# A fp32 hybrid decoder layer on one core: the embedding's early units loaded and split sooner, the second group's values built sooner and half by half, the last partial sum added in PSUM

## The chip, the core and the metric

One NeuronCore of a Trainium2 chip. The metric is device time of one execution in microseconds (us), lower is better. The engines are TensorE (PE; PEld is its weight load), VectorE (DVE), ScalarE (ACT), GpSimd (POOL) and SyncE (SP, which here only issues DMAs).

## The reference

One layer over 1024 tokens of width 2048, all in fp32:

```python
h = x @ w_in + b_in
q, k, v, g_attn, u_pool, g_pool = split(h)          # 16 heads of 64, 2 KV groups of 8 heads
a = banded_sink_attention(q, k, v, sinks, rel_bias) * silu(g_attn)   # window 128, blocks of 128
b = multiscale_pool(u_pool, w_pool, pool_scale) * silu(g_pool)       # trailing means 2, 4, 8, 16
mix = concat(a, b) @ w_out
ple = sigmoid(x @ w_gate_ple) * (p @ w_ple)         # p: (1024, 256), w_ple: (256, 2048)
out = layer_norm(sqrt(2) * x + mix + ple, gain, bias)
```

## The kernel before

**Matmuls.** A product of two fp32 matrices is made of three matmuls in the type fp32r (`mm3`, lines 182 to 184): each operand is split into hi (a cast on ScalarE, line 728) and lo (a subtraction on VectorE, line 125), and the matmuls are hi·hi, hi·lo and lo·hi. The big products run in groups of a Strassen-like scheme (`run_group`, `product`): a group has the seven products p1, p2, p5, p6, p7, p3, p4 in this order, each for up to three jobs, and each `product` is 12 matmuls of 512 columns. Its left operands are units of the input (b11, b21, t1 = sums of b12 and others, t2, t3, t4, b22, in hi and lo tiles such as `t1h`, `t1l`), its right ones slices of the weights (`raw`, sums of them in `s`, split into `wh`, `wl`). Units are loaded, summed and split some products ahead of their use (`units_to(i + 4)`).

**Order.** The code is written in the order of the work; `tick()` counts products, `after(t, f)` and `later(d, f)` hang a piece of work on a count. A tile scheduler then fixes the order of instructions on each engine. Within an engine, instructions run in order. SP's loads go out in order, and each waits for the landing of the load eight before it.

**The start.** `first()` in `run` loads the first operands. While they arrive, TensorE multiplies four of the embedding's eight units early (`EARLY = (0, 1, 6, 7)`; here n = 0 to 3): `ple_load` loads two units of `w_ple` at once into a `two` tile (512 KB), `ple_split(n)` splits one (casts on ScalarE at line 767, subtractions on VectorE) into the tiles that later hold t3 (`t3h`, `t3l`), and `ple_half(n, h)` multiplies one half of the tokens (12 matmuls; p lies in `t4h`, `t4l`) into the PSUM banks `tr` and `pv` and copies them to `b22h` or `b22l`. Units 2 and 3 (`ple_load(3)` loads both) are worked between the products of group 0: `turn` puts `ple_half(2, 0)`, (2, 1), (3, 0), (3, 1) ahead of the p5 products of the three jobs and of the first p6. `p5` products go to the PSUM bank `qb` and `sc`, p6 to `qa`.

**Heads.** A second part of the matmuls runs interleaved with the attention heads (`heads(h, j)`: 16 calls, two halves of the tokens, h, for each of 8 pairs). `v_build(g, src)` makes for each half h of the tokens a tile `v0` or `v1` from the stored values (`src`, loaded by POOL from `kv`): transposes on TensorE (line 522), a cast on ScalarE (524), a subtraction on VectorE; the products with the probabilities (line 625, into `pv`) read it. For KV group 0 it is made ahead of the heads, for group 1 in between, at tick t + 63 + 22, both halves from one call.

**The tail.** The last jobs are plain products (`run_plain`, 256 columns, F2). Their results are sums of a part in SBUF (`new_part`) and PSUM; `less_mean` (line 905) subtracts the mean with one more matmul. `norm_square` squares each block (ScalarE, line 915), `norm_scale` sums the squares on TensorE (924), makes 1/std (942 and a power on POOL) and spreads it over PSUM (957). `norm_out_two` multiplies eight pairs of blocks by it on VectorE, scales each by gain and bias (the pair's first block on ScalarE, its second on an engine that is given, line 975; `None` is ScalarE) and stores it (SP, 256 KB each).

Of the kernel before, what the change touches and what calls it, by code (L numbers as in the profile page):

```python
# [32 lines left out]
T = 512  # L33
# [7 lines left out]
Q0, KB, VB, GA0, U0, GP0 = 0, 8, 9, 10, 18, 26  # L41
# [23 lines left out]
class Layer:  # L65
# [80 lines left out]
    def fetch(self, src, extra=False):  # L146
        s = self.extra() if extra else self.slot()
        return self.load(s[:, : src.shape[-1]], src)
# [17 lines left out]
    def later(self, n, fn):  # L166

        def run():
            with ExitStack() as ctx:
                for ins in self.latest.values():  # L170
                    ctx.enter_context(self.tc.issue_after(ins))
                fn()
        self.after(n, run)
# [303 lines left out]

    def run_plain(self, g):

        (job,), order = self.groups[g]  # L480
        for i in range(2):
            ps = self.bank(BANKS[0][i], 2)[:, :F2]
            for u in range(2):
                wh, wl = self.take()
                for k in range(4):
                    f = slice(k * P, (k + 1) * P)
                    mm = self.mm3(ps, (wh[:, f], wl[:, f]), self.x_plain(4 * u + k), u + k == 0, False)
                if u:
                    mm = self.less_mean(ps, F1)
                self.mark("PE", mm)  # L490
                self.feed_raw()
                if u:
                    t = self.new_part(job.b[i])
                    self.add_to(t, ps, False)
                    job.done(job.b[i], t)
                self.tick()
# [17 lines left out]
    def v_build(self, g, src):  # L514

        nc = self.nc

        def build(h):
            vf = src[h]
            ps = self.bank(*((("tr", 1), ("sc", 2))[g and not h]), (P, 4, 2, 64))  # L520
            for i in range(4):
                nc.tensor.transpose(ps[:, i].rearrange("p g d -> p (g d)"), vf[:, i * P : (i + 1) * P], self.ident)
            v = self.vv[h] = self.tile(self.kv, [P, 4, P], f"v{h}", F32R)
            nc.scalar.copy(out=v[:, :, 0:64], in_=ps[:, :, g])
            self.lo(v[:, :, 64:128], ps[:, :, g], v[:, :, 0:64])

        for h in range(2):
            self.ident_act(src[h], src[h], self.c(C_BIN + VB))
            self.after(2 + (1 + 4 * g) * h, lambda h=h: build(h))

    def queries(self, j, c):
        self.ident_act(c, c, self.b8[:, j : j + 1], 0.125)
# [237 lines left out]
    def ple_half(self, n, h, tags):  # L770

        i = EARLY[n]
        if n > 1 and not h:
            self.ple_split(n)
        w = [t[:, n].rearrange("p (b k m) -> p b k m", b=2, k=2) for t in self.ple_w]
        ps = [self.bank(*tag) for tag in tags]
        with self.in_turn("PE"):
            for k in range(2):
                for b in range(2):
                    mm = self.mm3(ps[b], tuple(t[:, b, k] for t in w), tuple(t[:, 2 * h + k] for t in self.ple_p), k == 0, k == 1)  # L780
        self.turn["PE"] = mm.ins
        for b in range(2):
            out = self.copy(self.ple_out[(2 * n + b) % 4][:, h], ps[b])
        if not n:
            self.turn["ACT"] = out.ins
        for b in range(2):
            if h:
                self.aside(self.ple[2 * i + b], self.ple_out[(2 * n + b) % 4].rearrange("p h t -> p (h t)"))
# [193 lines left out]
    def run(self):  # L982
        nc, tc, fix = self.nc, self.tc, self.fix
# [28 lines left out]
        halves = lambda t: t.rearrange("p (h t) -> p h t", h=2)  # L1012
        store = lambda w: hid if w is win else gat
        qkv = [(win, *p) for p in [(KB, VB)] + pairs(Q0, 4)]
        ga, gp, u = ([(win, *p) for p in pairs(b, 4)] for b in (GA0, GP0, U0))
# [26 lines left out]
        def jobs(todo, half, first, done, tokens=2 * T, ahead=None):  # L1042
            return [Job(w, b0, b1, half, first(w), done(w), tokens, ahead=ahead) for w, b0, b1 in todo]
# [14 lines left out]
        for j in s5[-2:]:  # L1058
            j.filled = True
        s6 = [Job(w, b0, b1, 0, None, lambda b, c: self.second_done(b, c), F2, plain=True) for w, b0, b1 in centred]  # L1060
        for j in s4[-2:]:
            j.wait = 6
        self.add(*s1[:3])
# [12 lines left out]
        for o in reversed(BESIDE):  # L1076
            u = UNITS[o]
# [23 lines left out]
        def piece(job, t, f):  # L1101
            self.load(self.raw[job][t][:, f], job.w[job.b[t], job.half][:, f])

        lo, up, all_ = slice(0, H), slice(H, 2 * H), slice(0, 2 * H)
        def first(fetch, r):
            ple_p = self.ple_inputs()
            fetch("b11", 0)
            piece(s1[0], 0, lo)
            fetch("b11", 1)
            fetch("b11", 2)  # L1110
            piece(s1[1], 0, lo)
            piece(s1[2], 0, lo)
            piece(s1[0], 1, all_)
            piece(s1[0], 0, up)
            fetch("b21")
            piece(s1[1], 0, up)
            piece(s1[2], 0, up)
            fetch("b12")
            for job in s1[1:3]:
                piece(job, 1, all_)  # L1120
            fetch("b22")
            self.ple_load(3)
            self.load(self.cst, self.cst_src)
            self.ple_begin(ple_p)
            self.ple_half(0, 0, (("tr", 1), ("pv", 1)))
            self.ple_half(0, 1, (("qa", 2), ("qa", 2)))
            a, b = r["b11"]
            self.split_unit("b11", [])
            self.split_part("b11", 0, a[:, 0])
            self.units_to(1)  # L1130
            self.split_part("b11", 1, a[:, 1])
            self.ple_half(1, 0, (("qb", 2), ("qb", 2)))
            self.split_part("b11", 2, b)
            self.units_to(2)
            self.ple_half(1, 1, (("tr", 1), ("pv", 1)))
            self.units_to(3)
            self.turn.pop("ACT")
            self.three_sums(s1[0])
            self.units_to(4)

        begin, *steps = self.set_from(xs[0], T, kept, first)
        begin()
        turn = {(2, 0): (2, 0), (2, 1): (2, 1), (2, 2): (3, 0), (3, 0): (3, 1)}
        self.run_group(0, steps, before=lambda *at: at in turn and self.ple_half(*turn[at], (("tr", 1), ("pv", 1))))
        self.turn.clear()
        self.ident = fix.tile([P, P], F32, name="ident")
        make_identity(nc, self.ident)
# [11 lines left out]
        g = 2  # L1159
# [4 lines left out]
        self.slots = self.work_pool("slots", 16, work)  # L1164
        self.kv = self.work_pool("kv", 1, over)

        def build_kv(b, build, group):
            src = [self.slot()[:, :T] for h in range(2)]
            for h in range(2):
                self.aside(src[h], kvd[b][:, h * T : h * T + T])  # L1170
            self.later(2, lambda: build(group, src))

        t = 9
        self.after(5, lambda: build_kv(KB, self.k_build, 0))
        self.after(6, lambda: build_kv(VB, self.v_build, 0))
        for i in range(16):
            self.after(t - 2 + 9 * i, lambda i=i: self.heads(i % 2, i // 2))
        self.after(t + 63 + 8, lambda: build_kv(KB, self.k_build, 1))
        self.after(t + 63 + 22, lambda: build_kv(VB, self.v_build, 1))
        self.centre_weights(8, 3)  # L1180
        begin, *steps = self.set_kept(xs[0], kept)
        for i in range(1, n2):
# [84 lines left out]
        filled, turn = {}, []  # L1267
# [35 lines left out]
        for k in range(4):  # L1303
            r = rest_x[k]
            f = slice((k % 2) * 2 * F2, (k % 2) * 2 * F2 + 2 * F2)
            h, l = (t[k // 2][:, f].rearrange("p (k t) -> p k t", k=2) for t in (hi, lo))
# [28 lines left out]
        two = self.norm_begin(F2, F1, new)  # L1335
# [6 lines left out]
        self.drain()  # L1342
        self.norm_scale(two)
        for i, d in enumerate(pair):
            self.norm_out_two(two, 2 * i, d, (nc.gpsimd, None, nc.gpsimd, nc.vector, nc.gpsimd, None, nc.gpsimd, nc.vector)[i])
        tail.close()
        work.close()
        parts.close()
# [34 lines left out]
def build(nc, tc, a, out):  # L1383
    with ExitStack() as ctx:
        Layer(ctx, tc, a["x"], a["p"], a["win"], a["wgate"], a["wout"], a["wple"], a["wpool"], a["cst"], a["rel"], out).run()
# [15 lines left out]
```

## Time and profile before

| | us |
|---|---|
| median of 3 runs | 1479.01 (1477.32 to 1482.19) |
| profiled execution | 1477.94 |
| its span | 1476.2 |
| TensorE busy in the span | 1439.7 (98%) |
| VectorE, ScalarE, GpSimd busy | 1123.1 (76%), 788.4 (53%), 295.8 (20%) |
| mean granted TensorE clock | 0.993 |

The span is that of the profiled instructions; 1.74 us of the execution lie around it. Lines name the kernel's line (L184), the engine, the operation and out<-in by the program's names. A timeline's line has the start, the busy time, and in brackets the idle time before it with what ended it; a waits line has who waited, for whom, the total, the number of times and the longest.

### The profile page before, as it was taken

The numbers are of one execution on the slowest core, as the hardware profiler recorded it, in microseconds if no ns is written. First come the engines' busy times: TensorE is split into PE (matmuls) and PEld (weight loads), VectorE is DVE, ScalarE is ACT, GpSimd is POOL, SyncE is SP. The second block draws the span as 40 slices with busy tenths as digits, with TensorE's granted clock in tenths as the row PEclk, the third lists the DMA queues.
The fourth block names the chain that finished last, engine by engine and source line by source line (L and its number), as shares of the span: only waits on it lengthen the run. The fifth ranks groups of instructions, "written<-read, shape, count | busy, mean of one in ns | idle before, by whom it ended". The sixth has DMA issues, their size and how long they took to land. (4 is left out here: it accounts for less than half of the span.)

```text
span 1476.2 us, 20532 instructions
## 1 busy us (share of the span) xinstructions
PE 1439.7 (98%) x6928; PEld 1217.1 (82%) x6928; DVE 1123.1 (76%) x2033; ACT 788.4 (53%) x1566; POOL 295.8 (20%) x412
## 2 busy tenths in 40 slices
PE   8899999999999999999999999999999999999996
PEld 7788888888888788888788778788877888899995
DVE  6758577888788888888777786767678566987786
ACT  6535456655666566565655354433356433554475
POOL 1000113233233232324011111111011111111232
PEclk9899999999999999999999999999999999999998
DMA  9364687454445554466765759899699678595465
GB/s 350 145 215 170 164 230 232 145 170 165 158 173 181 185 169 171 172 214 218 205 198 133 207 160 307 288 266 289 196 320 301 168 190 231 138 258 126 120 239 200
DMA packets 109993, 301.35 MB, mean 204 GB/s; under 512 B 12544, under 2 KB 18048, under 8 KB 109888
## 3 DMA queue, kind: packets, MB, share of 16 engines
q1 hardware_dynamic: 84672, 217.46, 42.9%
q0 software_dynamic: 21888, 75.25, 21.0%
q10 hardware_dynamic: 3328, 7.34, 1.5%
q8 instruction: 54, 0.88, 0.2%
q14 instruction: 51, 0.42, 0.1%
HBM read 205.62 MB, written 94.37 MB: 203 GB/s over the span
## 5 line engine op out<-in xcount | busy, mean ns | idle before, releaser
L728 ACT CAST wh<-raw 128x512 fp32r<-128x512 f32 x428 | 264.1, 619 | 401.5 <-PE qa L183 132.5
L125 DVE TENSOR_TENSOR wl<-raw,wh 128x512 fp32r<-128x512 f32 x428 | 300.3, 705 | 111.2 <-ACT wh L728 105.4
L402 ACT COPY part<-qa 128x512 f32<-128x512 f32 (+1 forms) x180 | 103.9, 577 | 75.0 <-PE qa L184 74.0
L612 POOL TENSOR_SCALAR_AFFINE_SELECT s<-s 128x512 fp32r<-128x512 f32 x128 | 102.1, 809 | 132.2 <-ACT s L605 96.6
L125 DVE TENSOR_TENSOR part<-part,qb 128x512 f32<-128x512 f32 (+1 forms) x120 | 81.0, 675 | 44.9 <-PE qb L184 38.7
L182 PE MATMUL qa<-b11h,wh 128*128 128x512 f32 (+2 forms) x292 | 109.3, 374 | 0.4 <-ACT wh L728 0.4
L182 PE MATMUL qb<-b21h,wh 128*128 128x512 f32 (+2 forms) x292 | 109.1, 374 | 0.0
L184 PE MATMUL qa<-b11h,wl 128*128 128x512 f32 (+2 forms) x292 | 108.9, 373 | 0.0
L183 PE MATMUL qa<-b11l,wh 128*128 128x512 f32 (+2 forms) x292 | 108.8, 373 | 0.0
L184 PE MATMUL qb<-b21h,wl 128*128 128x512 f32 (+2 forms) x292 | 108.7, 372 | 0.0
L183 PE MATMUL qb<-b21l,wh 128*128 128x512 f32 (+2 forms) x292 | 108.5, 372 | 0.0
L182 PE MATMUL qa<-t2h,wh 128*128 128x512 f32 (+1 forms) x260 | 100.9, 388 | 3.3 <-ACT wh L728 2.1
L182 PE MATMUL qb<-t1h,wh 128*128 128x512 f32 (+1 forms) x260 | 101.2, 389 | 2.3 <-ACT t2h L728 1.4
L182 PE MATMUL qa<-t4h,wh 128*128 128x512 f32 (+1 forms) x260 | 100.4, 386 | 2.4 <-DVE part L125 2.4
L182 PE MATMUL qa<-t3h,wh 128*128 128x512 f32 (+1 forms) x260 | 100.6, 387 | 1.8 <-ACT part L402 1.8
L184 PE MATMUL qa<-t2h,wl 128*128 128x512 f32 (+1 forms) x260 | 100.1, 385 | 1.6 <-DVE wl L125 1.6
L182 PE MATMUL qb<-b22h,wh 128*128 128x512 f32 (+1 forms) x260 | 100.2, 386 | 0.0
L183 PE MATMUL qb<-t1l,wh 128*128 128x512 f32 (+1 forms) x260 | 100.0, 385 | 0.0
L184 PE MATMUL qb<-t1h,wl 128*128 128x512 f32 (+1 forms) x260 | 100.0, 385 | 0.0
L184 PE MATMUL qb<-b22h,wl 128*128 128x512 f32 (+1 forms) x260 | 99.8, 384 | 0.0
L183 PE MATMUL qa<-t3l,wh 128*128 128x512 f32 (+1 forms) x260 | 99.7, 384 | 0.0
L183 PE MATMUL qb<-b22l,wh 128*128 128x512 f32 (+1 forms) x260 | 99.7, 383 | 0.0
(325 smaller groups left out, 3577.1 us busy)
## 6 DMA issues: line engine op xcount, KB each, us to landing
raw<-in_win SPq DMA_DIRECT2D x65, 512.0 KB, 4.3
h<-part SPq DMA_DIRECT2D x34, 512.0 KB, 2.9
part<-h POOLq DMA_DIRECT2D x34, 512.0 KB, 6.6
cw<-in_wout SPq DMA_DIRECT2D x64, 256.0 KB, 3.0
raw<-in_wgate SPq DMA_DIRECT2D x32, 512.0 KB, 4.9
raw<-wc SPq DMA_DIRECT2D x32, 512.0 KB, 4.4
s<-in_x SPq DMA_DIRECT2D x44, 256.0 KB, 5.6
wc<-cw SPq DMA_DIRECT2D x32, 256.0 KB, 2.4
```

The lines of the kernel that those rows point to most:

```text
L125: return (eng or self.nc.vector).tensor_tensor(out=out, in0=a, in1=b, op=op)
L182: mm(ps, wh, xh, start=start, stop=False, skip_group_check=True)
L183: mm(ps, wh, xl, start=False, stop=False, skip_group_check=True)
L184: return mm(ps, wl, xh, start=False, stop=stop, skip_group_check=True)
L402: self.mark("ACT", self.nc.scalar.copy(out=dst, in_=ps))
L612: nc.gpsimd.affine_select(out=o4, in_=a4, pattern=[[0, 4], [sign, P]], compare_op=ALU.is_ge, fill=0.0, base=0 if side else -1, channel_mul ...
L728: ins = self.nc.scalar.copy(out=out, in_=a)
```

## The change

It has four parts. Lines of the changed kernel lie 8 to 16 higher behind the first edit.

1. `ple_load(3)` moves in SP's queue from behind b22 to ahead of b12, and `ple_split(2)`, `ple_split(3)` are called at group 0's position (1, 0), its second product, no more from `ple_half`.
2. Group 1's values are built in two calls, half 0 at tick t + 63 + 17 and half 1 at t + 63 + 24, each loading its own half of the source.
3. The last plain job's second block adds its stored part inside PSUM, by an fp32 matmul with the identity after the first of two units; ScalarE squares PSUM directly, and VectorE copies PSUM to the part beside it.
4. The second block of each of the eight last pairs is scaled on GpSimd (before: GpSimd four, ScalarE two, VectorE two times).

```diff
     def run_plain(self, g):
+            final = job.mean and i
...
+                if final and not u:
+                    t = self.new_part(job.b[i])
+                    nc.tensor.matmul(ps, self.ident, t, start=False, stop=False, skip_group_check=True)
                 if u:
                     mm = self.less_mean(ps, F1)
                 self.mark("PE", mm)
                 self.feed_raw()
-                if u:
+                if u and final:
+                    job.done(job.b[i], ps)
+                    nc.vector.tensor_copy(out=t, in_=ps)
+                elif u:
                     t = self.new_part(job.b[i])
                     self.add_to(t, ps, False)
                     job.done(job.b[i], t)
@@ v_build
-        for h in range(2):
+        for h in src:
             self.ident_act(src[h], src[h], self.c(C_BIN + VB))
-            self.after(2 + (1 + 4 * g) * h, lambda h=h: build(h))
+            self.after(2 + h * (g == 0), lambda h=h: build(h))
@@ ple_half
-        if n > 1 and not h:
-            self.ple_split(n)
@@ run
+        s6[-1].mean = True
...
             piece(s1[2], 0, up)
+            self.ple_load(3)
             fetch("b12")
             for job in s1[1:3]:
                 piece(job, 1, all_)
             fetch("b22")
-            self.ple_load(3)
...
-        self.run_group(0, steps, before=lambda *at: at in turn and self.ple_half(*turn[at], (("tr", 1), ("pv", 1))))
+        def early(*at):
+            if at in turn:
+                self.ple_half(*turn[at], (("tr", 1), ("pv", 1)))
+            elif at == (1, 0):
+                self.ple_split(2)
+                self.ple_split(3)
+
+        self.run_group(0, steps, before=early)
...
-        def build_kv(b, build, group):
-            src = [self.slot()[:, :T] for h in range(2)]
-            for h in range(2):
+        def build_kv(b, build, group, halves=(0, 1)):
+            src = {h: self.slot()[:, :T] for h in halves}
+            for h in halves:
...
-        self.after(t + 63 + 22, lambda: build_kv(VB, self.v_build, 1))
+        for h in range(2):
+            self.after(t + 63 + 17 + 7 * h, lambda h=h: build_kv(VB, self.v_build, 1, (h,)))
...
-            self.norm_out_two(two, 2 * i, d, (nc.gpsimd, None, nc.gpsimd, nc.vector, nc.gpsimd, None, nc.gpsimd, nc.vector)[i])
+            self.norm_out_two(two, 2 * i, d, nc.gpsimd)
```

What this does to the engines' order, in three places. In the names, numbers tell buffers apart; `two_152` and `two_153` are b12's halves and become t1, `two_203` and `two_204` are t2's halves.

VectorE at the start, before, from its row 17 on (the subtractions into `t3l` stand at rows 39 and 43, out of this piece):

```order
L125 TENSOR_TENSOR b21l_193_458<-two_155_319,b21h_192_457 128x1024
L125 TENSOR_TENSOR two_152_308<-two_156_324,two_152_308 128x1024
L125 TENSOR_TENSOR wl_196_482<-raw_145_295,wh_195_481 128x512
L125 TENSOR_TENSOR two_153_309<-two_157_325,two_153_309 128x1024
L125 TENSOR_TENSOR wl_199_500<-raw_147_297,wh_198_499 128x512
L125 TENSOR_TENSOR t1l_202_518<-two_152_308,t1h_201_517 128x1024
```

and after, from the same row:

```order
L125 TENSOR_TENSOR b21l_193_458<-two_155_319,b21h_192_457 128x1024
L125 TENSOR_TENSOR wl_196_482<-raw_145_295,wh_195_481 128x512
L125 TENSOR_TENSOR t3l_162_338<-two_156_324,t3h_161_337 128x512 x2
L125 TENSOR_TENSOR two_152_308<-two_157_326,two_152_308 128x1024
L125 TENSOR_TENSOR wl_199_500<-raw_147_297,wh_198_499 128x512
L125 TENSOR_TENSOR two_153_309<-two_158_327,two_153_309 128x1024
L125 TENSOR_TENSOR t1l_202_522<-two_152_308,t1h_201_521 128x1024
```

Both subtractions into `t3l` have moved ahead of the sums of t1, some twenty rows up.

ScalarE at the start, before, from its row 32 on:

```order
L767 CAST t3h_161_337<-two_160_334 128x512 x2
L728 CAST wh_213_576<-s1_212_571 128x512
L728 CAST wh_220_622<-raw_143_293 128x512
L728 COPY b22h_165_341<-tr_216_596 128x512
L728 COPY b22h_165_341<-pv_217_597 128x512
L728 CAST t2h_218_612<-two_203_523 128x1024
L728 CAST t2h_218_612<-two_204_526 128x1024
```

and after, from its row 31 on:

```order
L736 CAST t1h_201_521<-two_153_309 128x1024
L736 CAST t2h_218_614<-two_203_527 128x1024
L736 CAST wh_209_557<-s1_208_552 128x512
L736 CAST t2h_218_614<-two_204_530 128x1024
L736 COPY b22h_165_341<-tr_216_598 128x512
L736 COPY b22h_165_341<-pv_217_599 128x512
L736 CAST wh_213_580<-s1_212_575 128x512
```

The two copies that empty `tr` and `pv` after `ple_half(2, 0)` stood ahead of the casts into `t2h`, and now stand behind them.

TensorE around the first use of group 1's `v0`, before, from its row 2174 on; the first use follows 13 rows behind the transposes, at row 2189:

```order
L603 MATMUL tr_1001_4909<-ident_972,s_936_4552 128x128 x2
L603 MATMUL tr_1001_4909<-ident_972,s_949_4627 128x128 x2
L522 MATMUL sc_1006_4934<-ident_972,s_972_4760 128x128 x4
L182 MATMUL qa_1012_4948<-b11h_326_1273,wh_988_4829 128x512
L183 MATMUL qa_1012_4948<-b11l_327_1274,wh_988_4829 128x512
```

and after, from its row 2094 on, with the first use at row 2189 as before:

```order
L575 MATMUL sc_969_4737<-kh_410_1759,s_958_4675 128x256
L575 MATMUL sc_969_4737<-kl_411_1760,s_958_4675 128x256
L530 MATMUL sc_970_4744<-ident_972,s_940_4577 128x128 x4
L182 MATMUL qa_963_4687<-t2h_346_1377,wh_953_4642 128x512
L183 MATMUL qa_963_4687<-t2l_347_1378,wh_953_4642 128x512
```

The four transposes moved from row 2176 to row 2096, 80 rows up.

More of the change, by code (lines that the diff above doesn't have):

```diff
@@ L478, in run_plain @@
     def run_plain(self, g):
+        nc = self.nc
         (job,), order = self.groups[g]
```

## The prediction

> **What bounds the kernel.** I read the page's busy line first, then TensorE's own waits, then a table of windows, then the timeline around the longest waits.
>
> ```profile
> span 1476.2 us, 20532 instructions
> PE 1439.7 (98%) x6928; PEld 1217.1 (82%) x6928; DVE 1123.1 (76%) x2033; ACT 788.4 (53%) x1566; POOL 295.8 (20%) x412
> ...
> PE tr L184 <- DVE t3l L125: 5.3, 1, 5.3
> PE tr L182 <- ACT t3h L767: 2.3, 1, 2.3
> PE pv L625 <- DVE v L125: 1.7, 1, 1.7
> ```
>
> TensorE is busy for all but 36.5 us, so only its idle time, its clock and the work that it is given can change the end. The last three lines (us in total, times, longest) are its three longest waits inside the span: two on the early embedding unit, one on the second group's values. The change is aimed at just these and at the tail.
>
> ```profile
> 34.17:37.58 3.41, 1.20 (x4) 0.67 (x4) 3.41 (x6) 1.66 (x3) 2.95 (x1) 1.00 0.50 189
> 37.58:41.00 3.42, 0.00 (x0) 0.00 (x0) 3.42 (x7) 1.14 (x2) 0.00 (x0) 0.50 0.31 96
> 41.00:44.41 3.41, 2.15 (x5) 1.77 (x6) 3.41 (x5) 0.00 (x0) 0.00 (x0) 0.50 0.00 0
> 44.41:47.82 3.41, 3.41 (x9) 2.64 (x9) 3.34 (x5) 2.24 (x4) 0.00 (x0) 0.50 0.56 226
> 47.82:51.24 3.42, 3.42 (x16) 2.82 (x16) 3.42 (x4) 2.04 (x3) 0.00 (x0) 1.00 0.98 388
> 60.00:420.00 360.00, 360.00 (x1713) 301.34 (x1712) 275.62 (x561) 206.18 (x450) 73.47 (x94) 1.00 0.56 177
> ```
>
> Columns: window, length, busy time of PE, PEld, DVE, ACT, POOL, granted clock, DMA share, GB/s. VectorE is full from 34.17 to 44.41 while TensorE starves: the start is bound by the order of VectorE's queue. The two waits also cost the clock, 0.50 for three windows. From 60 on TensorE never stops, so what the start saves reaches the end. This execution took 1477.94 us; the median of the runs is 1479.01, 1.07 above. A change within 0.3% (4.4 us) is about what a measurement cannot tell from none.
>
> **Part 1, the early embedding units.**
>
> ```profile
> 22.79 0.33 SPq L139 DMA_DIRECT2D two<-in_wple  x1
> two<-in_wple SPq DMA_DIRECT2D x1, 512.0 KB, 11.4
> 26.21 1.23 DVE L125 TENSOR_TENSOR two<-two,two 128x1024 f32<-128x1024 f32 x1 [3.02 <-DMA two<-in_x]
> 27.47 1.05 ACT L728 CAST t1h<-two 128x1024 fp32r<-128x1024 f32 x1 [2.29 <-DVE two L125]
> 33.09 0.39 PE L184 MATMUL sc<-b21h,wl 128*128 128x512 f32 x1
> 34.37 1.22 DVE L125 TENSOR_TENSOR two<-two,two 128x1024 f32<-128x1024 f32 x1
> 35.09 1.13 ACT L767 CAST t3h<-two 128x512 fp32r<-128x512 f32 x2
> 35.51 0.68 DVE L125 TENSOR_TENSOR raw<-raw,raw 128x512 f32<-128x512 f32 x1
> 35.75 0.50 PE L182 MATMUL tr<-t4h,t3h 128*128 128x512 f32 x1 [2.28 <-ACT t3h L767]
> 36.11 0.68 DVE L125 TENSOR_TENSOR wl<-s,wh 128x512 fp32r<-128x512 f32 x1
> 42.26 0.80 PE L184 MATMUL tr<-t4h,t3l 128*128 128x512 f32 x1 [5.31 <-DVE t3l L125]
> 44.80 0.59 ACT L728 COPY b22h<-tr 128x512 f32<-128x512 f32 x1 [4.35 <-PE tr L184]
> 54.28 0.39 PE L182 MATMUL qb<-t1h,wh 128*128 128x512 f32 x1
> 63.12 0.39 PE L182 MATMUL qa<-t2h,wh 128*128 128x512 f32 x1
> ```
>
> The wple load was issued at 22.79 and landed 11.4 later, at 34.2. Six 512 KB loads stand between its new and its old place; the first lands at 26.2 (VectorE's row at 26.21 waits for it). So one load lands each (34.2 − 26.2)/6 = 1.33 us. The unit now lands at 26.2, and b12, the two weight halves and b22 each one place later, by about 1.3 us: b12's halves at 27.6 and 28.9, b22's at 32.8 and 34.2.
>
> TensorE needs the matmuls from 33.32 (0.23 after 33.09) up to p6's first (63.12). They are seven groups of twelve, four of them early halves and three p5 products: 84 × 0.227 (39 matmuls from the row at 54.28 to the one at 63.12) = 19.1 us. With no wait at all p6 would start at 52.4 instead of 63.1, so the ceiling of this part is 10.7 us: 2.43 and 5.31 of waiting and the rest slow clock.
>
> Now the new waits. VectorE takes 0.60 for a 512 row (35.51 to 36.11) and 1.14 for a 1024 row (34.37 to 35.51). The unit lands at 26.2, ScalarE's two casts follow by 27.4 (1.13), and VectorE's two t3l by 28.1: five us ahead of TensorE's first use at 33.3, so both old waits go. Behind t3l VectorE never rests. Up to two_204, the half that the last t2h cast reads, stand five 1024 rows and seven 512 rows: 28.1 + 5.7 + 4.2 = 38.0, and 1.2 for itself, 39.2. The t2h cast follows on ScalarE (1.05 a row of 1024, at 27.47), and only then, at 40.2 to 40.3, the copy that frees PSUM's tr for the second half of unit 2, 0.59. Before, that copy stood ahead of the t2h casts. TensorE finishes p5's first product at about 39.05 (33.32 + 12 × 0.227 = 36.04, 0.28 more for VectorE's addition that frees its bank, 12 × 0.227) and stands until 40.84: 1.8 us. Behind it the other splits are ahead of TensorE by my walk along the three queues. So p6 starts at 40.84 + 60 × 0.227 = 54.5, and part 1 gains 63.1 − 54.5 = **8.65 us** (10.71 − 0.28 − 1.78). Bounds: 10.7 above; below, whatever a longer version of the new wait takes (first rival).
>
> The clock decides next. The four matmuls of 34.17 to 37.58 (1.20 us of 3.41, 35%) were followed by the drop. Another window further on was kept at full clock:
>
> ```profile
> 846.50:849.91 3.41, 1.87 (x8) 1.08 (x7) 3.41 (x7) 1.22 (x3) 0.00 (x0) 1.00 1.05 202
> ```
>
> That one held 1.54 us of idle time and was 55% busy (1.87 of 3.41). The window 37.58 to 41.00 of the changed kernel would hold the 1.8 us gap, thus 1.6 of 3.41, 47%, between the two and nearer to the kept one. I take no drop.
>
> The Trainium skill, "TensorE: Matmul & The Clock Gate", Part 1, puts the drop behind at least one idle window of about 3.4 us, and its table "Why this matters for your kernels" asks for no gaps over about 3 us; by that the 1.8 us gap is harmless and the sum stands. The trace is harsher than this: its clock fell 0.6 us into the second gap, after a window with four matmuls in it, so the page settles nothing at 47%.
>
> **Part 2, the values, half by half.**
>
> ```profile
> 445.60:487.49 41.89, 41.89 (x206) 34.84 (x206) 35.67 (x86) 24.75 (x66) 14.63 (x18) 1.00 0.58 201
> 460.81 0.64 PE L625 MATMUL pv<-s,v 128*128 128x256 f32 x4
> 484.15 0.60 PE L522 MATMUL sc<-ident,s 128*128 128x128 f32 x4
> 488.68 0.42 DVE L125 TENSOR_TENSOR v<-sc,v 128x256 fp32r<-128x256 f32 x1
> 489.24 0.47 PE L625 MATMUL pv<-s,v 128*128 128x256 f32 x2 [1.75 <-DVE v L125]
> ```
>
> Before, v0's four transposes stand 13 matmul rows ahead of the first use, and the cast and the subtraction sit behind other work on their queues. Now 93 rows lie between, some 20 us (206 matmuls and their like fill 41.89, 0.20 each, and most of these are full ones), and the chain transposes, cast, subtraction needs 489.1 − 484.15 = 5 us. The old v0 is read last at 460.81, the new transposes come at about 467.5, so nothing stands against the earlier write. The 1.75 us wait goes; next to be late would be v1, moved three ticks earlier too. The cost is a cast on ScalarE and 0.42 on VectorE in an earlier place, and POOL's load of the source half now stands ahead of four mask operations (AFFINE_SELECT), where a wait for its slot would hold softmax. In 445.60 to 487.49 TensorE is busy throughout and POOL for 14.63 of 41.89, so I put it at nothing, with 1.75 as the worst (the whole gain returned). Gain **1.75**, 0 to 1.75.
>
> **Part 3, the last partial sum.**
>
> ```profile
> L931 PE MATMUL sc<-csum,ones x4: 592/592/592, 1304.5 to 1305.8; 128*128 128x512 f32 x4
> 1461.46 0.42 DVE L125 TENSOR_TENSOR t1h<-t1h,qb 128x256 f32<-128x256 f32 x1 [1.56 <-PE qb L905]
> 1461.97 0.42 ACT L915 ACTIVATE t2l<-t1h 128x256 f32<-128x256 f32 x1 [2.53 <-DVE t1h L125]
> ```
>
> The addition leaves the chain, and the square starts where it did: 1461.97 − 1461.46 = 0.51 saved. The added matmul is plain fp32, whose rows of 512 columns stand (1305.8 − 1304.5)/3 = 0.43 apart, so two instructions of 256 cost about 0.44 on a TensorE that has no idle time there. The copy beside the square (0.42) is done before scaling starts at 1465.8. Net gain **0.07**, from −0.4 (0.59 each instead of 0.22) to 0.5.
>
> **Part 4, the last scaling.**
>
> ```profile
> 1466.69 0.56 POOL L975 TENSOR_SCALAR t1h<-t1h,cst 128x256 f32<-128x256 f32 x1 [2.64 <-DVE t1h L125]
> 1471.05 0.41 DVE L975 TENSOR_SCALAR t2h<-t2h,cst 128x256 f32<-128x256 f32 x1
> 1469.00:1471.00 2.00, 0.00 (x0) 0.00 (x0) 2.00 (x4) 1.85 (x5) 1.14 (x2) 0.50 0.94 307
> 1471.00:1473.00 2.00, 0.00 (x0) 0.00 (x0) 0.42 (x2) 0.93 (x2) 0.07 (x1) 0.50 1.04 344
> 1471.50 1.00 SPq L139 DMA_DIRECT2D out<-t2h  x2
> out<-t2h SPq DMA_DIRECT2D x2, 256.0 KB, 3.0
> ```
>
> From 1469 the DMA engines are full (0.94, 1.04), so eight stores of 256 KB drain at 0.26 MB / 0.344 = 0.76 each whatever feeds them. GpSimd's eight at 0.56 follow VectorE's multiplications (0.60 apart for a 512 row, as above) and end near 1471.5, about when the last issue stood before. I give **0.2** for two fewer operations on VectorE ahead of its multiplications (2 × 0.41, mostly behind the full DMA), from −0.5 to 0.4.
>
> The Trainium skill, "GPSIMD Engine Reference", 4.1 Engine selection, advises against GpSimd for elementwise work, about twice slower than VectorE for two inputs and near line rate for one. At twice 0.41 the eight would take 6.6 us and end near 1473.3, some 1.5 later than I count, and the sum would be 1.7 us worse; the measured 0.56 is 1.4 times, and by that I count.
>
> **Sum.** 8.65 + 1.75 + 0.07 + 0.2 = 10.7 less; from 1477.94 that is 1467.3 for such an execution, and **1468.4** on the median of 1479.01.
>
> **Rivals.** *The new wait is dearer (18%).* The t2h casts hold the copy longer, or the clock falls after the 47% window. A half clock for one full window costs 1.7 us, for two 3.4; before, it took a fully busy window (44.41 to 47.82) to bring the clock back. That gives 1470.1 to 1471.8; with a wait of 3 us besides, 1473. For it: the copy now stands behind a cast that waits for VectorE, and VectorE has no slack. Against it: 47% is nearer to 55% than to 35%.
>
> *The gain is not kept (6%).* The head start would be lost to a later wait that hangs on DMA and not on TensorE's own progress, and the time stays within 4.4 us of 1479, about 1476. For it: DMA is full around 47.82 to 51.24 (0.98). Against it: TensorE did not stop once in the 360 us behind, with DMA at 0.56.
>
> *Slower (3%).* ScalarE and VectorE work in order, and both t3l now stand ahead of b12's sums. If wple lands late, every split behind it waits as long. My walk gives p6 at 56.3 for a landing at 28, 58.3 for 30, 62.4 for the old 34.2: one for one. The whole change breaks even at a landing near 36.9, and is slower by 0.3% from 41.3, thus 1483.5 there. Against it: loads land in the order of issue, 1.33 apart, and this one is moved forward by six places.
>
> **How the numbers follow.** My case, a gain of 9 to 12.5 us, has 73%: 1466.5 to 1470. Up to 1473.5 the first rival is taken in, and down to 1465.0 the ceiling of part 1 with the best of the others (10.7 + 1.75 + 0.5 + 0.4 = 13.4, to 1465.7) and a little for the spread of the runs (1477.32 to 1482.19). Faster by over 0.3%: 73 + 18 = 91%. Within it: 6%. Slower: 3%.
>
> **What the profile after would show.** Right: no wait of TensorE for t3h or t3l; one of about 1.8 us for ScalarE's b22h copy near 39 to 41, at clock 1.00; p6's first matmul at about 54.5; no 1.75 us wait for v near 479; POOL eight times at 0.6 in the tail. It is wrong if clock 0.50 stands anywhere between 30 and 60, if new waits for wl or t1h rows stand at 28 to 36 (b12 one place later was then not free), if a POOL or pv wait grows around 450 to 470, or if the last store issues later than ten us behind the old 1471.5 shifted forward.

## The result, and the profile after

| | before | after |
|---|---|---|
| median of 7 runs each | 1475.34 us (1472.72 to 1482.19) | 1468.62 us (1467.10 to 1471.58) |
| ratio, 95% interval | | 0.9946 (0.9932 to 0.9960) |
| the profiled execution, its span | 1477.94, 1476.2 | 1470.93, 1469.2 |

The changed kernel is faster by 0.54%, which is 8.0 us of 1475.3 (5.9 to 10.0). A second timing of five runs gave 0.9938 (0.9925 to 0.9952), 9.2 us. The forecast was 10.6. That the median of 1468.6 fell on the forecast 1468.4 is partly luck: four more runs of before brought its own median down from 1479.01 to 1475.34.

The waits of TensorE that answer to the three shown of before (who waited, for whom, total, times, longest):

```profile
PE sc L963 <- DVE t2l L125: 1.5, 1, 1.5
PE tr L182 <- ACT b22h L736: 1.4, 1, 1.4
```

The waits for t3h, t3l and v are gone. In their place stands the forecast wait for the copy that empties `tr`, 1.4 us. The other line is the tail's, which was there before. The start of after in TensorE's timeline, and two windows:

```profile
35.93 0.47 PE L182 MATMUL qb<-t1h,wh 128*128 128x512 f32 x1 [0.38 <-DVE part L125]
40.34 0.50 PE L182 MATMUL tr<-t4h,t3h 128*128 128x512 f32 x1 [1.44 <-ACT b22h L736]
54.11 0.39 PE L182 MATMUL qa<-t2h,wh 128*128 128x512 f32 x1
...
36.94:40.35 3.41, 1.97 (x10) 1.32 (x8) 3.41 (x6) 1.77 (x4) 0.00 (x0) 1.00 0.66 220
30.00:60.00 30.00, 28.19 (x123) 22.70 (x122) 27.96 (x35) 20.20 (x31) 2.98 (x5) 1.00 0.65 254
```

p6 starts at 54.11 (forecast 54.5, before 63.12). Even the least busy stretch of 3.41 us, 36.94 to 40.35, is 58% busy, and the clock column is 1.00 throughout.

The values and what comes behind them, then the tail:

```profile
478.31 0.40 PE L633 MATMUL pv<-s,v 128*128 128x256 f32 x2
488.65 0.33 PE L575 MATMUL sc<-kh,s 128*128 128x128 f32 x1 [0.36 <-DVE s L125]
489.37 0.33 PE L575 MATMUL sc<-kh,s 128*128 128x128 f32 x1 [0.28 <-DVE s L125]
...
1455.61 0.38 ACT L921 ACTIVATE t2l<-qb 128x256 f32<-128x256 f32 x1 [2.50 <-PE qb L911]
1459.89 1.67 POOL L981 TENSOR_SCALAR t1h<-t1h,cst 128x256 f32<-128x256 f32 x3 [2.24 <-DVE t1h L125]
1463.39 1.15 POOL L981 TENSOR_SCALAR t2h<-t2h,cst 128x256 f32<-128x256 f32 x2
1462.00:1464.00 2.00, 0.00 (x0) 0.00 (x0) 1.89 (x4) 2.00 (x5) 1.83 (x5) 0.50 1.04 339
1464.00:1466.00 2.00, 0.00 (x0) 0.00 (x0) 0.00 (x0) 0.53 (x1) 0.55 (x1) 0.50 1.04 343
```

The first product with the new v0 starts without a wait, but ten us on two score products wait 0.36 and 0.28 us, where before there was none. ScalarE squares the PSUM bank 0.38 after the last matmul's start (1455.23); before, it was 1461.97 − 1461.13 = 0.84. GpSimd's operations are 0.56 each, and the stores fill the DMA (1.04).

Matching the two traces matmul by matmul, after is ahead by 9.0 us at p6, 10.9 behind the first use of v0, 5.9 at 1460, and 7.0 at the last store. (Counted here and below are the matmuls of the products, lines 182 to 184, which are the same 6012 from p6 on in every kernel.) So 5 us went between 490 and 1460, in steps of 0.3 to 1.7; 0.43 of them is part 3's added matmul. The rest was the open question.

### The profile page after: what moved, and what is told of

Its sections match the earlier page's. It is cut to its first block, busy times and chain, and to the rows that moved or that the text cites. A ratio compares the mean times of both kernels' runs of the same rounds, so it can differ in the third digit from the quotient of the medians.

```text
span 1469.2 us, 20535 instructions
## 1 busy us (share of the span) xinstructions
PE 1437.4 (98%) x6930; PEld 1214.9 (83%) x6930; DVE 1120.8 (76%) x2031; ACT 787.3 (54%) x1564; POOL 294.4 (20%) x416
## 5 line engine op out<-in xcount | busy, mean ns | idle before, releaser
L184 PE MATMUL qa<-t4h,wl 128*128 128x512 f32 (+1 forms) x260 | 99.7, 384 | 0.0
L183 PE MATMUL qa<-t2l,wh 128*128 128x512 f32 (+1 forms) x260 | 99.7, 383 | 0.0
```

Of the source, the lines that this page charges most:

```text
L183: mm(ps, wh, xl, start=False, stop=False, skip_group_check=True)
L184: return mm(ps, wl, xh, start=False, stop=stop, skip_group_check=True)
```

## The experiments

**Is the loss in the middle of the run the kernel's or the execution's?** The changed kernel again, unaltered.

> The changed kernel unaltered, profiled and timed once more. In the first pair of traces TensorE was 10.9 us ahead at 489 us and only 5.9 at 1460. Theory (scatter): the 5 us came from transfers that happened to land later in that execution, so a second trace gives them back at other places, by an amount between 0 and 6 us, and the ratio over more rounds goes to (1475.3 - 11)/1475.3 = 0.9925 or so. Rival (structure): the same waits at the same places (a score product on DVE s near 488, a partial sum near 944, a p5 product near 1140), each of the same size within 0.2 us, and the ratio stays at 0.9946.

1469.09 against 1478.02, ratio 0.9938 (0.9925 to 0.9952). p6 at 53.17. The largest of the steps, a wait of 1.7 us near 944, is absent from this trace, so its size was that execution's own. A wait near 1139 is there again (1.35 us, 1.23 in the first trace). It turned out to be in eleven of the study's twelve traces (0.73 to 1.35 us), and the one without it is the first trace of before: that one had been lucky there. The loss as a whole came back, though: from the 1800th matmul behind p6 to the 5990th the two traces of after take 936.4 and 935.9 us, the two of before 932.7 and 933.4, so 3.7 us are lost in the first pair and 2.5 in the second, in part at other places. Neither account holds alone. This is the wait in the second trace of before:

```profile
1147.18 0.50 PE L182 MATMUL qb<-t1h,wh 128*128 128x512 f32 x1 [1.35 <-DVE part L125]
```

**Part 1 alone.**

```diff
             piece(s1[2], 0, up)
+            self.ple_load(3)
             fetch("b12")
...
+                self.ple_split(2)
+                self.ple_split(3)
```

> Before with only the embedding's load and splits moved. Theory: p6's first matmul at 54.1, the lead of 9.0 us at 60 reaches the end; ratio 0.994 (1475.3 - 9). Rival (a stretch bound by DMA takes the lead away, whichever part made it): 9.0 at 60, 4 to 5 left at the end, ratio 0.997.

Ratio 0.9950 (0.9937 to 0.9963), 7.4 us. p6 at 53.37. Between the two accounts in time, nearer to the first.

**Part 2 alone.**

```diff
-        self.after(t + 63 + 22, lambda: build_kv(VB, self.v_build, 1))
+        for h in range(2):
+            self.after(t + 63 + 17 + 7 * h, lambda h=h: build_kv(VB, self.v_build, 1, (h,)))
```

> Before with only group 1's values built earlier, half by half. Theory: the wait of 1.75 us for v goes, nothing comes in its place but up to 0.6 us on a score product near 497; 1.2 to 1.75 us faster, ratio 0.999. Rival (the earlier values delay the heads behind them): the lead is lost again by 550 and the ratio is 1.000 to 1.002.

Ratio 0.9989 (0.9979 to 0.9998), 1.6 us. In the trace the wait for v is gone and a score product waits 0.28.

**Parts 3 and 4 alone.**

```diff
+        s6[-1].mean = True
...
+            self.norm_out_two(two, 2 * i, d, nc.gpsimd)
```

> Before with only the tail changed: the last part added in PSUM and GpSimd scaling eight blocks. From the first pair of traces 0.5 us up to the last sum of squares and 0.25 behind it, so 0.75 us faster, ratio 0.9995, below what this measurement can tell; the trace decides, from the last product (L905) to the last landing of a store. Rival (the added matmul costs what it saves): 0.0 to 0.3 us.

Ratio 0.9993 (0.9983 to 1.0003): not distinguishable, as expected. The trace tells more:

```profile
1458.99 0.28 PE L913 MATMUL qb<-two,w 128*128 128x256 f32 x1
1459.37 0.38 ACT L923 ACTIVATE t2l<-qb 128x256 f32<-128x256 f32 x1 [2.50 <-PE qb L913]
1463.52 1.67 POOL L983 TENSOR_SCALAR t1h<-t1h,cst 128x256 f32<-128x256 f32 x3 [2.12 <-DVE t1h L125]
```

0.38 again from the last matmul to the square (0.84 before). From the first store's landing to the last it is 5.34 us here as in the four other traces with part 4 (5.34 to 5.36), and 5.60 to 5.62 in the seven without. From the last product to the last landing it is 12.7 us here and 13.4 in the second trace of before, so 0.7 is saved there. (In the first trace of before it is 14.0, in load late too: in both the clock fell only 3.0 to 3.2 us behind the last product.) The price of part 3 lies ahead of that stretch. These are two matmuls of the products, in after and in before; between them stands one more of the products (left out here), and in after the added one, L492:

```profile
1453.27 0.28 PE L184 MATMUL qb<-b11h,wl 128*128 128x256 f32 x1
1453.39 0.59 PE L492 MATMUL qb<-t1h,ident 128*128 128x256 f32 x2
1453.93 0.28 PE L183 MATMUL qb<-b21l,wh 128*128 128x256 f32 x1
```

```profile
1459.60 0.28 PE L184 MATMUL qb<-b11h,wl 128*128 128x256 f32 x1
1459.84 0.28 PE L183 MATMUL qb<-b21l,wh 128*128 128x256 f32 x1
```

The two stand 0.66 us apart with it and 0.24 without, and all five traces with part 3 show the same 0.43 of difference. So the two parts together save about 0.3 us. That is the rival's figure: the expected 0.75 had left out the added matmul.

**The same kernel twice, and the halves of part 1.** Before once more; the load moved alone; the splits called earlier alone; the load just ahead of b22.

> The kernel before, unaltered, profiled and timed once more: how far two traces of one kernel differ. From p6's first matmul to the last product the three traces without part 1 took 1397.6 to 1397.9 us, the three with it 1400.2 to 1401.0. Theory (scatter): this one may fall anywhere in 1397 to 1401. Rival (part 1 costs something later): it falls at 1397.6 to 1398.2 again. Ratio 1.000 by both.

Ratio 1.0005 (0.9993 to 1.0017). p6 at 61.22 against 63.12 in the first trace: the start itself varies by 2 us. From p6 to the last product it took 1398.5 us, just above the rival's stretch and low in the theory's, so this one trace decides neither.

```diff
# load_only: before, and
+            self.ple_load(3)
             fetch("b12")
```

> Before with the wple load alone moved ahead of b12; the splits stay called from ple_half. The scheduler then places both t3l where the whole part has them (row 19 of VectorE). Theory (the load's place decides): p6 at 53.2 to 54.2, as with all of part 1, ratio 0.994 to 0.995. Rival (the earlier call of the splits decides): p6 stays near 62.

Ratio 0.9953 (0.9935 to 0.9970), p6 at 53.55: all of part 1's gain. The earlier call of the splits adds nothing once the load is early: TensorE, VectorE, ScalarE and GpSimd have the same order as in part 1 alone, row for row.

```diff
# split_only: before, and
+                self.ple_split(2)
+                self.ple_split(3)
```

> Before with the splits alone called earlier; the load stays behind b22. Both t3l move from rows 39 and 43 of VectorE to row 31, t3h stays. Theory: the wait for t3h (1.3 to 2.9 us) stays, the one for t3l shrinks from 5.3 to about 1.1 (VectorE is through with row 30 at 36.8, two t3l by 38.0), the clock still falls but for one window; p6 at about 57.5, ratio 0.997. Rival (a late load holds VectorE's queue, my slower case): p6 at 62 or later, ratio 1.000 or above.

Ratio 0.9973 (0.9962 to 0.9984), p6 at 55.09. TensorE's two waits, VectorE's t3l and the two windows around the waits, against the second trace of before:

```profile
34.66 0.50 PE L182 MATMUL tr<-t4h,t3h 128*128 128x512 f32 x1 [0.84 <-ACT t3h L767]
36.35 0.50 PE L184 MATMUL tr<-t4h,t3l 128*128 128x512 f32 x1 [0.96 <-DVE t3l L125]
35.62 1.29 DVE L125 TENSOR_TENSOR t3l<-two,t3h 128x512 fp32r<-128x512 f32 x2
31.35:34.77 3.42, 2.58 (x12) 1.80 (x12) 3.42 (x6) 1.30 (x3) 0.54 (x1) 1.00 0.95 378
34.77:38.18 3.41, 2.45 (x10) 1.71 (x11) 3.41 (x6) 0.36 (x1) 3.41 (x1) 1.00 0.73 249
```

```profile
40.07 0.69 DVE L125 TENSOR_TENSOR t3l<-two,t3h 128x512 fp32r<-128x512 f32 x1
40.81 0.79 PE L184 MATMUL tr<-t4h,t3l 128*128 128x512 f32 x1 [5.31 <-DVE t3l L125]
```

With the load as late as before, eight and eleven rows of VectorE's queue are worth 4.4 us of waiting on t3l and, in this trace, the clock of the start. I expected a fall of the clock there for one window; there was none, but one came later, at 481.91 (see the clock below). By time the gain is 4.0 us (2.4 to 5.6) of the 7.4 that all of part 1 gave. So what cost most of the time at the start was t3l's row in VectorE's queue. The load's place matters because the scheduler moves the split with it: t3l stands at row 19 with the load landing at 23 to 25, at 26 with 30.5, at 31 with 33.9. That the scheduler goes by landing times is read from these rows alone.

```diff
# load_late: part 1, but
             for job in s1[1:3]:
                 piece(job, 1, all_)
+            self.ple_load(3)
             fetch("b22")
```

> Part 1 with the load placed just ahead of b22 (landing near 31.6 instead of 23 to 25). My walk, with the queues' order held fixed, gave 2.0 us of delay for each 2 us of later landing, so p6 near 59.8. Theory now: the scheduler puts t3l seven rows lower on VectorE (row 26 instead of 19), where the data are there when its turn comes; p6 at 54 to 55 and ratio 0.995.

Ratio 0.9950 (0.9932 to 0.9968). The load lands at 30.54, over five us later than in after, and p6 comes at 52.96, the earliest of the study:

```profile
31.64 1.28 DVE L125 TENSOR_TENSOR t3l<-two,t3h 128x512 fp32r<-128x512 f32 x2
39.21 0.50 PE L182 MATMUL tr<-t4h,t3h 128*128 128x512 f32 x1 [0.59 <-ACT b22h L728]
```

My slope of one for one is refuted as a statement on this kernel: when the load is moved, the queue is rearranged with it.

**The new waits behind the values.** The changed kernel with half 1 called three ticks later, at its old rows; then that with the late load.

```diff
-            self.after(t + 63 + 17 + 7 * h, ...
+            self.after(t + 63 + 17 + 10 * h, ...
```

> The changed kernel with half 1 of the values called at tick t + 63 + 27 instead of 24, which puts v1's transposes, cast and subtraction back to their old rows; half 0 stays early. Theory: v1's cast (0.37) and subtraction (0.42), which now stand ahead of the queries' splits, make the score products near 489 wait 0.36 + 0.28 us; with v1 back these waits go, and the v wait of 1.75 stays away, so 0.5 to 1.0 us less between p6 and the 1800th product behind it. Rival (the wait comes from the load of the source on GpSimd's queue or from v0): the waits stay. Ratio 0.993 to 0.994, no difference to the changed kernel that a time can show.

1467.45, ratio 0.9940 (0.9925 to 0.9955). One wait is gone, one stays:

```profile
486.82 0.33 PE L575 MATMUL sc<-kh,s 128*128 128x128 f32 x1
487.54 0.33 PE L575 MATMUL sc<-kh,s 128*128 128x128 f32 x1 [0.28 <-DVE s L125]
```

But the second trace of the unaltered changed kernel shows the same picture, 0.28 alone. So v1's place is not what makes the 0.28, and whether it made the 0.36 isn't shown. From p6 to the 1800th matmul behind it, it is 461.6 us here and 461.7 and 461.4 in the two traces of after, so the expected 0.5 to 1.0 did not come: a miss. What makes the 0.28 stands on VectorE in the same trace:

```profile
485.19 0.84 DVE L125 TENSOR_TENSOR s<-pv,s 64x256 f32<-64x256 f32 x2
486.02 1.46 DVE L125 TENSOR_TENSOR s<-s,s 64x512 fp32r<-64x512 f32 x2
```

The second of the two subtractions for the queries is through at 487.48, and the score product starts at 487.54. TensorE now arrives earlier than that.

> As the one before, and the wple load just ahead of b22, where p6 came earliest (52.96). Expected: p6 at 52.9 to 53.6 against 53.2 to 54.1, score products without a wait, ratio 0.993 (1476.9 less 10.3). If the middle gives back 1.5 to 2 us whenever the start is early, 0.994.

1468.94, ratio 0.9941 (0.9927 to 0.9956), p6 at 53.83, later than expected, and a score product waiting 0.28, where none was expected. No better than the changed kernel beyond the scatter.

**What all twelve traces say on the middle.** From p6's first matmul to the last product, and the part of it from the 1800th matmul behind p6 to the 5990th (row starts, in us):

| | from p6 to the last product | from the 1800th to the 5990th |
|---|---|---|
| no part 1: before, again, part 2 alone, parts 3 and 4 alone | 1397.9, 1398.5, 1397.6, 1397.8 | 932.7, 933.4, 933.4, 932.5 |
| early start, values as before: part 1 alone, load only, load late, split only | 1400.4, 1399.9, 1396.5, 1400.9 | 934.4, 934.5, 931.5, 934.1 |
| early start, values early: after, again, v1 later, both moved | 1401.0, 1400.2, 1397.7, 1399.4 | 936.4, 935.9, 933.2, 934.8 |

The means of the first column are 1398.0 for four and 1399.5 for the eight, which reach from 1396.5 to 1401.0. It holds what parts 2 and 3 change and, in split only, a fall of the clock; the second column lies clear of these, with means of 933.0 and 934.4. Up to the 1200th matmul all twelve take 295.8 or 295.9 us; behind it they part. That an early start gives back 1.4 us on average is possible, and the timings (7.4, 6.9 and 7.4 us with part 1, the load alone and the late load, against 8.6 at p6) lean that way; but load late and v1 later, with the same early start, gave little or nothing back in their traces. Part 1 alone and load late have the same order on every engine behind the start, and their middles differ by 3.9 us. The three pairs with one and the same order throughout (before, after, part 1 alone with load only) differ by 0.5 to 0.8. So how much of the difference is scatter between executions isn't settled, and no mechanism was found for it.

## Why the prediction was right, point by point

**Part 1, 8.65 us.** Right in mechanism and in size: p6 stood at 63.12, 61.22, 62.77 and 61.05 in the four traces without part 1 (mean 62.0), and at 54.11, 53.17, 53.37 and 53.13 with all of it (53.4): 8.6. The load landed at 25.1 in the first trace of after and about 23 in two others, against 26.2 in my working. The new wait for the copy behind the t2h cast is there, in the order read from the queues: 1.44, 0.75, 0.45 us where I had 1.78, and under 0.2 in one. An earlier landing may have shortened it, but this isn't shown: load only, landing at 24.0, waited 1.13 us, and load late, landing at 30.5, only 0.59. The other two sub-steps were not needed: the splits' call adds nothing, and the slope of the slower rival was wrong.

**The clock.** "I take no drop" came true: nowhere in 30 to 60 us did the clock fall with an early start. But the ground for it, that 47% of matmuls is near enough to the kept 55%, does not hold, and this step was luck. In each trace the changes of the clock lie on a grid of 3.41 us (before: 37.58 and 47.82, three windows apart; split only: 481.91 and 485.32, one apart). So the windows of this grid are the ones to read. In split only such a window held 47% of matmuls, around the wait for v, and the clock fell behind it for a whole window; so it did behind 1.35 us (39%) in part 2 alone, the last two lines:

```profile
481.19 0.47 PE L625 MATMUL pv<-s,v 128*128 128x256 f32 x2 [1.80 <-DVE v L125]
478.50:481.91 3.41, 1.61 (x10) 1.14 (x10) 3.38 (x7) 3.38 (x9) 1.34 (x2) 1.00 0.82 329
481.91:485.32 3.41, 3.41 (x10) 2.76 (x10) 2.22 (x9) 2.06 (x9) 1.96 (x3) 0.50 0.36 112
32.37:35.78 3.41, 1.35 (x6) 0.77 (x5) 3.41 (x6) 0.32 (x1) 0.32 (x1) 1.00 0.69 282
35.78:39.20 3.42, 2.07 (x4) 1.16 (x4) 3.42 (x6) 1.33 (x3) 2.57 (x1) 0.50 0.57 191
```

It held in load late and in after:

```profile
476.36:479.78 3.42, 1.67 (x11) 1.24 (x10) 3.39 (x8) 3.40 (x9) 1.45 (x3) 1.00 0.73 292
38.67:42.08 3.41, 1.97 (x10) 1.42 (x9) 3.41 (x7) 2.88 (x5) 0.00 (x0) 1.00 0.39 156
```

Over all twelve traces it fell behind every window of the grid at full clock with up to 1.61 us of matmuls, and held with 1.73 (51%) or more; in between it held once, with the 1.67 above, and fell at the end of three traces, with 1.70. So about half a window decides here. After held because its wait for b22h was 1.44 us: with the forecast 1.8 its window would by estimate have kept 1.97 − 0.36 = 1.6 us, as much as the one in split only behind which the clock fell. The fall needs no idle window: a wait of 1.80 us was enough. The Trainium skill, "TensorE: Matmul & The Clock Gate", Part 1, asks for one idle window of about 3.4 us; the traces differ from it, as the first did. The fall in split only cost 1.5 us: the next eight matmuls took 3.38 us, in the eleven other traces 1.83.

The times of before go with the clock too: of its 55 executions timed beside the experiments, the three with a mean clock of 0.991 took 1479.7 us on average, the three with 0.996 took 1474.2; the twelve of after had 0.995 to 0.997.

**Part 2, 1.75 us.** The wait for v went, the gain did not stay whole. The step that failed is "next to be late would be v1": it is the split of the queries on VectorE, 0.28 to 0.64 us of waiting, and the score products of this place spread out. From the 1200th to the 1800th matmul behind p6 the five traces with early values take 165.6 to 165.9 us, and the three with neither part 1 nor early values 166.5 to 166.8: 0.9 us, and 1.6 (0.3 to 3.1) by time. Beside an early start part 2 is worth more: with the values as before part 1 alone, load only and load late take 166.7 to 167.7 there, 1.4 us longer on average. And the wait that it removes can cost the clock as well, as in split only, one of the seven traces that have it.

**Part 3, 0.07 us.** Right in both terms: 0.84 − 0.38 = 0.46 saved (0.51 in the working), and the added matmul cost 0.43 (0.44), so 0.03 are left.

**Part 4, 0.2 us.** 5.61 − 5.35 = 0.26 from the first landing to the last. The slower case, in which twice VectorE's time would have cost 1.5 us (from its own figures, 1473.3 against 1471.5, it is 1.8), did not come: GpSimd took 0.56 us, 1.4 times VectorE's 0.41, and the stores' DMA set the pace, as its window of 1.04 shows. The Trainium skill's "GPSIMD Engine Reference", 4.1 Engine selection, gives about that factor for two inputs and near line rate for one; this operation has one, and its 1.4 lies between.

**The sum.** 8.6 + 0.9 + 0.03 + 0.26 = 9.8 us by the traces' stages (10.3 with part 2's 1.4 beside an early start), and 7.4 + 1.6 + 1.0 = 10.0 by the parts' times; the whole measured 8.0 and 9.2. The forecast of 10.7 had taken part 2 whole. The step "From 60 on TensorE never stops" is shown for 60 to 420 alone: between 420 and 1461 TensorE of before stood idle for 14.8 us, and it is there that the traces part. Some of the lead may be lost there, which isn't settled.

## What to carry to other kernels

Where a wait is long, look for the row of the engine's queue at which the awaited instruction stands: moving the t3l splits up by about ten rows on a full VectorE gained seven of the 8.6 us at p6 in its trace, and 4.0 of 7.4 by time, without moving a byte earlier. Here moving a load moved the queues too, so a slope read from a fixed order did not hold for the next version. And compare two traces of the same kernel before explaining a difference: here up to 2 us at the start, single waits of 1.3 to 1.7 us, and 0.8 us over the 1400 us of the middle lay between two such traces. When the price of an added instruction is measured, the stretch must begin ahead of it.

## What the runs showed of the hardware

The granted clock changed on a grid of 3.41 us. It fell behind grid windows with matmuls still in them: 1.20 us in the first trace of before, 1.35 in part 2 alone, 1.61 (47%) in split only, where the one wait was 1.80 us long. It held behind 1.67 (49%) once and behind all with 1.73 or more. An fp32 matmul of 256 columns, two instructions long, cost 0.43 us between matmuls of 256 columns that stand 0.12 apart. And the time between the same two matmuls of the products, 6011 of them apart, differed by 3.9 us between two kernels with one and the same order there, through waits of up to 1.7 us whose lengths and places differed.
